# Alternating the two DMA rings between loads and stores, tile by tile, in a split SiLU-multiply kernel

## The chip, the cores and the metric

The kernel runs on one core of one Trainium2 chip. The metric is the device time of one execution in microseconds (us), as the median of several runs; lower is better. Beside the timed runs there is one profiled execution, from which the page of the profile, its views and the record of DMA packets come. Times inside it are counted from the start of its span.

## The reference

The input `x` is a float32 array of 32 x 512 x 2048 (134.22 MB). Each row of 2048 is cut in two halves of 1024; the output is the SiLU of the first half times the second half, in float32, 32 x 512 x 1024 (67.11 MB).

```python
x1, x2 = x[..., :half_dim], x[..., half_dim:]
silu_x1 = x1 * (1 / (1 + np.exp(-x1)))
return (silu_x1 * x2).astype(np.float32)
```

## The kernel before, in words

**Tiling.** The 16384 rows are cut into 16 tiles. A tile has 128 partitions with K = 8 rows each, so a load brings 128 x 16384 floats (8.39 MB) and a whole store takes away 128 x 8192 floats (4.19 MB). A partition's part of a tile is contiguous in the device memory: 64 KB of input and 32 KB of output. In the document `L5` is the load of tile 5 and `S5` its store.

**Buffers.** There are two input buffers, `xt0` and `xt1`, and two output buffers, `ot0` and `ot1`; tile `i` uses number `i % 2` of each. So `L(i+2)` must wait until the multiply of tile `i` has read `xt`, and the multiply of tile `i+2` must wait until `S(i)` has left `ot`.

**Compute.** `compute(i)` issues the SiLU on ScalarE (ACT, L96, in place in the first half of the tile) and then the multiply on VectorE (DVE, L102, into `ot`). Tile 0 is cut into four chunks and tile 15 into three (`LAST`, of 2, 3 and 3 rows); the others are one chunk.

**Transfers.** All of them go through `move` (L77). SyncE (SP) and ScalarE each own a ring on which their DMAs are queued; the page calls the ring of SP q1 and the ring of ACT q10. In the kernel before, every load is issued by SP and every store by ACT. A store on ACT stands in ACT's own instruction stream between the SiLU of its tile and the SiLU of the next tile. `S0` is cut into three pieces by partitions (`OPENING`), and `S15` into three pieces by rows, in step with `LAST`; they are called `S15a`, `S15b` and `S15c` here.

**Order of the work.** The schedule is written out by hand (`manual_schedule`). After `compute(i)` the loop issues `S(i)` and `L(i+2)`, both of which wait for the multiply of tile `i`. Which of the two is written first changes every four tiles (`load_first`); that decides only the order in which the transfers take their eight completion semaphores. At the end `settle_all_but` puts a nop on SP (L67) that waits for the completion of all transfers but the last one, so that what remains after it is the wait for `S15c` and the closing barrier (L160). The calls to `implied` tell the scheduler which dependencies follow from others already waited for.

Of the kernel before, what the change touches and what calls it, by code (L numbers as in the profile page):

```python
# [1 line left out]

# [4 lines left out]


@with_exitstack
def kernel(  # L10
    ctx: ExitStack,
    tc: tile.TileContext,
    x: bass.AP,
    out: bass.AP,
):


    nc = tc.nc
    P = nc.NUM_PARTITIONS

    x_flat = x.flatten_outer_dims()
    out_flat = out.flatten_outer_dims()
    num_rows, in_cols = x_flat.shape
    half = in_cols // 2
    dt = x_flat.dtype

    K = 8
    FIRST = [2] * (K // 2)
    LAST = [2, 3, 3]
    OPENING = [  # L30
        (slice(0, None, 4), slice(None)),
        (slice(2, None, 4), slice(None)),
        (slice(1, None, 2), slice(None)),
    ]
    RUN = 2
    n_tiles = num_rows // (P * K)

    pool = ctx.enter_context(tc.tile_pool(name="pool", bufs=1))
    xts = [pool.tile([P, K, in_cols], dt, name=f"xt{b}") for b in range(2)]
    ots = [pool.tile([P, K, half], dt, name=f"ot{b}") for b in range(2)]  # L40

    def view(flat, i):
        return flat.rearrange("(g p t k) d -> g t p k d", p=P, t=RUN, k=K)[i // RUN, i % RUN]

    ctx.enter_context(tc.manual_schedule(engines={mybir.EngineType.Activation, mybir.EngineType.DVE}))

    sent = []
    loads, stores, silus, muls = {}, {}, {}, {}

    def implied(later, earlier, reason):  # L50
        for x in later:
            for y in earlier:
                tc.declare_no_dep(x, y, reason=reason)

    def earlier(done, i):
        return [ins for j in range(i % 2, i, 2) for ins in done[j]]

    def after(later, first):
        tc.add_manual_dep(
            later,  # L60
            first.name,
            mybir.DependencyInfo(mybir.DependencyClass.NoSync, mybir.DependencyReason.DATA),
            reason="order in which the transfers take their semaphores",
        )

    def settle_all_but(n, others):
        rest = nc.sync.nop(nofuse=True)  # L67
        for ins in sent[:-n] + others:
            tc.add_manual_dep(
                rest.ins,  # L70
                ins.name,
                mybir.DependencyInfo(mybir.DependencyClass.Sync, mybir.DependencyReason.DATA),
                reason="sync sees each earlier transfer land before the last ones",
            )

    def move(queue, out, in_):
        ins = queue.dma_start(out=out, in_=in_).ins  # L77
        sent.append(ins)
        return ins

    def load(i):
        loads[i] = [move(nc.sync, xts[i % 2][:], view(x_flat, i))]
        if i >= 2:
            implied(loads[i], earlier(loads, i), "the multiplies that this load awaits came after those loads")
            implied(loads[i], earlier(silus, i), "the multiplies that this load awaits came after those activations")

    def parts(sizes):
        assert sum(sizes) == K
        return [slice(sum(sizes[:n]), sum(sizes[:n + 1])) for n in range(len(sizes))]

    def compute(i, ot, chunks):
        xt = xts[i % 2]
        silus[i], muls[i] = [], []
        for ks in chunks:
            silus[i].append(
                nc.scalar.activation(  # L96
                    out=xt[:, ks, :half],
                    in_=xt[:, ks, :half],
                    func=mybir.ActivationFunctionType.Silu,
                ).ins  # L100
            )
            muls[i].append(nc.vector.tensor_mul(out=ot[:, ks], in0=xt[:, ks, :half], in1=xt[:, ks, half:]).ins)  # L102
        implied(muls[i], loads[i], "each multiply awaits an activation that came after the load")
        if i >= 2:
            implied(silus[i], earlier(silus, i), "the load that this activation awaits came after those activations")
            implied(silus[i], earlier(muls, i), "the load that this activation awaits came after those multiplies")
            implied(muls[i], earlier(muls, i), "the store that this multiply awaits came after those multiplies")

    def store(i, ot, pieces):
        ov = view(out_flat, i)  # L110
        stores[i] = [move(nc.scalar, ov[ps, ks], ot[ps, ks]) for ps, ks in pieces]

    ALL = slice(None)
    load(0)
    load(1)
    for i in range(n_tiles):
        ot = ots[i % 2]
        last = i == n_tiles - 1
        compute(i, ot, parts(FIRST if i == 0 else LAST if last else [K]))
        pieces = [(ALL, ALL)]  # L120
        if i == 0:
            pieces = OPENING
        elif last:
            pieces = [(ALL, ks) for ks in parts(LAST)]
        load_first = i // 4 % 2
        if load_first and i + 2 < n_tiles:
            load(i + 2)
        store(i, ot, pieces)
        if load_first and i + 2 < n_tiles:
            after(stores[i][0], loads[i + 2][0])  # L130
        if not load_first and i + 2 < n_tiles:
            load(i + 2)
            after(loads[i + 2][0], stores[i][-1])
    settle_all_but(1, muls[n_tiles - 1])


# [1 line left out]
_INS = ['x']  # L138
_OUTS = [((32, 512, 1024), 'float32')]


# [23 lines left out]
```

## Time and profile before

| what | value |
|---|---|
| time, median of 3 runs | 471.06 us (470.71 to 471.17) |
| span of the profiled execution | 469.2 us |
| what lies around the span, as median less span | 1.9 us |
| VectorE busy | 139.5 us (30%) |
| ScalarE busy | 114.2 us (24%) |
| moved by DMA | 201.33 MB, mean 429 GB/s over the span |
| share of 16 DMA engines, ring q1 (loads) and q10 (stores) | 66.4% and 33.2% |
| from issue to landing, whole load and whole store (median) | 42.2 us and 42.0 us |

The profiled execution has no separate time of its own beside the span; the 1.9 us around the span are the difference to the median of the runs. An engine's busy time is a share of the span. A queue's share is the time that its packets took, summed and divided by 16 engines' span, so the two shares together say how full the DMA engines were.

### The profile page before, as it was taken

Reading aid. Unit: us, or ns where it says so; the run is one execution under the profiler, and the core shown is the slowest. Engines: PE = TensorE matmul, PEld = TensorE weight load, DVE = VectorE, ACT = ScalarE, POOL = GpSimd, SP = SyncE. Lnnn points to the kernel's source line nnn. Section 1 sums busy time; section 2 is a strip of 40 time slices with the busy share of each in tenths; the row PEclk is TensorE's granted clock in tenths of the full one; section 3 lists DMA queues with packets and bytes.
Section 4 is the critical chain, followed back from the end, with each engine's and each line's share of the span. In section 5 each row is a group of like instructions: output and inputs, shape, how many; then the busy total and the mean of one; then the engine's idle time right before and its main releaser. Section 6 shows DMA issues by size and latency. Waiting matters only on the chain.

```text
span 469.2 us, 156 instructions
## 1 busy us (share of the span) xinstructions
DVE 139.5 (30%) x21; ACT 114.2 (24%) x22; POOL 0.2 (0%) x4
## 2 busy tenths in 40 slices
DVE  0070522407034070330704307042070520605152
ACT  1051405032050410504105050050501405014060
POOL 0000000000000000000000000000000000000000
DMA  8999999999999999999999999999999999999998
GB/s 358 447 447 374 475 402 433 416 492 402 411 439 486 408 402 447 475 419 402 444 439 458 402 436 413 492 402 416 433 486 408 402 447 475 419 402 444 450 402 358
DMA packets 4928, 201.33 MB, mean 429 GB/s; under 512 B 576, under 2 KB 576, under 8 KB 576
## 3 DMA queue, kind: packets, MB, share of 16 engines
q1 hardware_dynamic: 2304, 134.22, 66.4%
q10 hardware_dynamic: 2624, 67.11, 33.2%
HBM read 134.22 MB, written 67.11 MB: 429 GB/s over the span
## 4 chain that ended last, share of the span: by engine, by line
DMA 72%; DVE 14%; ACT 11%; DVEq 1%; issue 0%; SPq 0%
DMA xt<-in_x_dram 72%; DVE ot L102 14%; ACT xt L96 11%; DVEq L160 1%; SPq L77 0%
## 5 line engine op out<-in xcount | busy, mean ns | idle before, releaser
L102 DVE TENSOR_TENSOR ot<-xt 128x8192 f32<-128x8192 f32 (+2 forms) x21 | 139.5, 6659 | 320.8 <-ACT xt L96 320.8
L96 ACT ACTIVATE xt<-xt 128x8192 f32<-128x8192 f32 (+2 forms) x21 | 112.9, 5400 | 341.4 <-DMA xt<-in_x_dram 341.4
L96 ACT ACT_TABLE_LOAD x1 | 1.3, 1283 | 0.7 <-PEq L149 0.7
L149 POOL MEMSET const-bfloat16-1.0<- 128x1 bf16 x1 | 0.1, 102 | 0.0
L149 POOL MEMSET const-uint8-127<- 128x1 uint8 x1 | 0.1, 102 | 0.0
L149 POOL MEMSET const-float32-0.0<- 128x1 f32 x1 | 0.1, 99 | 0.2 <-issue 0.2
L149 POOL MEMSET const-float32-1.0<- 128x1 f32 x1 | 0.1, 99 | 0.0
## 6 DMA issues: line engine op xcount, KB each, us to landing
out_dram<-ot ACTq DMA_DIRECT2D x14, 4096.0 KB, 42.0
out_dram<-ot ACTq DMA_DIRECT2D x3, 1024.0 KB, 12.0
out_dram<-ot ACTq DMA_DIRECT2D x2, 1536.0 KB, 7.9
out_dram<-ot ACTq DMA_DIRECT2D x1, 2048.0 KB, 37.2
xt<-in_x_dram SPq DMA_DIRECT2D x16, 42.2
```

Source lines behind the costliest of these rows:

```text
L96: nc.scalar.activation(out=xt[:, ks, :half], in_=xt[:, ks, :half], func=mybir.ActivationFunctionType.Silu,).ins
L102: muls[i].append(nc.vector.tensor_mul(out=ot[:, ks], in0=xt[:, ks, :half], in1=xt[:, ks, half:]).ins)
L149: nc = _bacc.Bacc("TRN2", target_bir_lowering=False, num_devices=1)
L160: with _tile.TileContext(nc) as tc:
```

## The change

The helper `load` issues the loads of tiles 3, 5, ..., 15 on ScalarE instead of SyncE, and `store` issues the stores of odd tiles (1, 3, ..., 15, the last in three pieces) on SyncE instead of ScalarE. `L0` and `L1`, the loads of even tiles, and the stores of even tiles stay where they were. For an odd tile's load the declaration about earlier activations falls away, as that load now stands behind those activations on their own engine.

The ring of SP then holds L0, L1, L2, S1, L4, S3, L6, S5, ..., L14, S13, S15a, S15b, S15c, and the ring of ACT holds S0 (three pieces), L3, S2, L5, S4, ..., L15, S14.

```diff
     def load(i):
-        loads[i] = [move(nc.sync, xts[i % 2][:], view(x_flat, i))]
+        loads[i] = [move(nc.scalar if i >= RUN and i % 2 else nc.sync, xts[i % 2][:], view(x_flat, i))]
         if i >= 2:
             implied(loads[i], earlier(loads, i), "the multiplies that this load awaits came after those loads")
-            implied(loads[i], earlier(silus, i), "the multiplies that this load awaits came after those activations")
+            if not i % 2:
+                implied(loads[i], earlier(silus, i), "the multiplies that this load awaits came after those activations")
...
     def store(i, ot, pieces):
         ov = view(out_flat, i)
-        stores[i] = [move(nc.scalar, ov[ps, ks], ot[ps, ks]) for ps, ks in pieces]
+        stores[i] = [move(nc.sync if i % 2 else nc.scalar, ov[ps, ks], ot[ps, ks]) for ps, ks in pieces]
```

## The prediction, made before the changed kernel was run

> **What bounds the kernel now.** I read the page first: the span, the busy shares, and how full the DMA engines are.
>
> ```profile
> span 469.2 us, 156 instructions
> ...
> DVE 139.5 (30%) x21; ACT 114.2 (24%) x22; POOL 0.2 (0%) x4
> ...
> DMA  8999999999999999999999999999999999999998
> ...
> q1 hardware_dynamic: 2304, 134.22, 66.4%
> q10 hardware_dynamic: 2624, 67.11, 33.2%
> ```
>
> No compute engine is busy for a third of the span, while the two rings together fill 66.4 + 33.2 = 99.6% of the 16 DMA engines. The page's chain of waits says "DMA 72%; DVE 14%; ACT 11%", which looks like a latency loop (load, SiLU, multiply, next load). It isn't one that costs anything: the table of windows, over two tiles each, shows full DMA engines at one constant rate while that loop turns.
>
> ```profile
> 116.86:174.86 58.00, 17.38 (x2) 14.06 (x2) 0.00 (x0) 1.00 1.00 434
> 348.86:406.86 58.00, 17.38 (x2) 14.06 (x2) 0.00 (x0) 1.00 1.00 434
> ```
>
> The last columns are the DMA share (1.00) and GB/s (434). Two tiles are 25.17 MB, and 25.17 MB / 58.00 us is 434 GB/s: the period of 29 us a tile is set by bytes. So I looked at single packets. The DMA view of three short windows, each catching one round of 16 packets (one on each engine; the share is summed duration / 16 engines / window, so with a window of 1 us it is the mean duration in units of 0.01 us):
>
> ```profile
> q1 hardware_dynamic: 16, 1.05, 241.8%
> ...
> q10 hardware_dynamic: 16, 0.52, 121.3%
> ...
> q1 hardware_dynamic: 16, 1.05, 328.3%
> ```
>
> The first (48 to 49 us) is a normal load packet: 64 KB in 2.418 us. The second (39.5 to 40.5) is a store packet: 32 KB in 1.213 us. The third (36 to 37) is the round just before the ring of ACT carries its first packet: 3.283 us instead of 2.418, so 0.87 us too long. I come back to it. In the packet record the engines take one load packet and one store packet in turn, 3.62 us a round, from 62 to 448 us without a gap. Packet times add up to 466.6 us an engine, and the DMA engines run from 1.73 to 468.04 us. Nothing is left between packets.
>
> The end, from the timeline:
>
> ```profile
> 435.92 0.34 ACTq L77 DMA_DIRECT2D out_dram<-ot  x1
> 449.08 4.56 ACT L96 ACTIVATE xt<-xt 128x2048 f32<-128x2048 f32 x2 [21.91 <-DMA xt<-in_x_dram]
> ...
> 453.35 0.34 ACTq L77 DMA_DIRECT2D out_dram<-ot  x1
> ...
> 457.07 3.60 ACTq L77 DMA_DIRECT2D out_dram<-ot  x2
> ```
>
> L15 lands at 449.06; S14, S15a, S15b and S15c are issued at 435.92, 453.35, 457.07 and 460.33. In the packet record S14's last packets end at 457.68 to 458.27, S15a's run until about 460.5, S15b's and S15c's until 468.04: each piece is issued 3 us or more before its first packet can go. The end, too, is set by bytes, not by the chain.
>
> **The change, part by part.**
>
> *Issuing instructions.* Seven loads go from SP to ACT, and seven whole stores and three pieces from ACT to SP: SP issues 19 transfers instead of 16, ACT 17 instead of 20. One costs 0.33 us on SP and 0.34 to 0.36 on ACT in the timeline. What hides them is the backlog: L(i+2) and S(i) are issued when L(i+1) and S(i-1) still have 13.1 us to go (L15 lands at 449.06, S14 is issued at 435.92). Without that cover it would be some 0.03 us a tile, 0.5 us in all. I take 0.
>
> *What is queued behind the moved instructions.* On ACT an odd tile's load waits for the multiply (8.69 us) just where the store waited, and behind it stands the next SiLU, whose load lands 13 us later. On SP, S3 waits for the multiply of tile 3, and behind it stands L6, which needs a later multiply anyway. The added waits on older transfers' semaphores (L5 on a piece of S0, for instance) find transfers that landed over 30 us before; an event wait takes 0.02 to 0.03 us in the record. POOL and DVE issue nothing. 0 us.
>
> *The order on the DMA engines.* This is the part that could matter. Each transfer is 8 packets and one semaphore write on each engine, so nine turns, load or store alike. Before, the pairs that share the engines are (L2, S0), (L3, S1), (L4, S2) and so on: L(i+2) and S(i) are issued together, run side by side and land within 0.2 us (L14 at 420.11, S12 at 419.94). After the change L3 stands behind S0 and S1 behind L2; as L2 and S0 end in the same round (72.12 and 71.94), L3 and S1 start together again, and with nine turns on both rings the offset stays the same through the kernel. Every pair is the pair of before, with its rings swapped for odd tiles. Neither ring runs empty before L15 ends. Inside a pair of odd tiles the load's packet now goes ahead of the store's (1.21 us earlier), but its semaphore write takes its turn after the store's last packet, so L15 lands 0.2 us earlier at most, which the backlog swallows. 0 us.
>
> *The end.* S13 ends with L15, near 449 us, and the ring of SP is then empty until S15a is issued at about 453.4, while S14 runs on the ring of ACT with three packets left. From there S14 and S15a take turns, then S15a, S15b and S15c follow. The bytes are the same and both rings hold work, so the last packet again ends near 468.0, unless waking an idle ring costs something: rival 1.
>
> *The nop on SP.* It now stands behind the issue of S15c (460.7) rather than waiting since 409. Its last condition, S15b, lands at 464.74, and S15c at 468.38; its few event waits (0.13 us for the last two) fit in between. Without that cover they would cost about 0.2 us. 0 us.
>
> The sum is 0 for a span of 469.2, and with the 1.9 us around it 471.1 us.
>
> **The rivals.**
>
> *1. Waking an idle ring stalls the engines (slower).* The ring of ACT wakes once in the trace: S0 is issued at 33.5, and the load round before its first packet is stretched by 0.75 to 1.05 us (mean 0.87), though another load packet was queued. The very first packets of the kernel are stretched alike (up to 3.445 us). Before the change there is no other wake. After it, SP's ring is woken by S15a in a stretch where the engines have no slack, so the whole stall goes into the end: 471.06 + 0.87 = 471.9, at most 472.1. For it: the only wake in the trace shows it. Against it: the stall may belong to the first use of a ring or to the first write in the kernel, and both happen alike in both kernels. [...]
>
> *2. Mixing directions on one ring costs something at each change (slower).* Before, each ring carries one direction only, so the trace can't show a load behind a store on the same ring. What it shows is that engines change direction at every packet for nothing (2.418 and 1.213 us throughout), and that the turn from one pair to the next costs 0.01 to 0.02 us (rounds of 3.63 and 3.64 against 3.62). After the change, 14 such turns change direction on a ring. It decides from 0.94 / 14 = 0.07 us a turn on. At the stall of rival 1 each time it would be 14 x 0.87 = 12 us, 483 us; at a tenth of that 1.2 us, 472.3. The bound below is 0: a turn can't get cheaper than the 0.02 us that it costs.
>
> *3. Faster.* That would need shorter packets, since start (1.73 us), end (1.15 us) and the two stretched rounds lie outside what is changed. Taking 0.2% off means 5 ns of each 2418 ns packet, perhaps because on a ring that alternates the read of the next packet meets the write of the one ahead less often; 470.1. Nothing in the trace varies by that much: 1926 of 2048 load packets took 2.418 us to the nanosecond. [...]
>
> That the change doesn't do what it says can be put aside: the instruction streams built from it hold the rings as listed above.
>
> **How the numbers follow.** No change, 471.1 us (470.5 to 471.7): 0.54. Rival 1, 471.9 to 472.1: 0.26. Rival 2, from 472.0 up: 0.14. Rival 3: 0.06. A difference of 0.2%, 0.94 us, is about the least that a measurement of this kernel can tell from none. Rival 1 at 0.75 to 1.05 us lies across that bound, so I split it in halves: within 0.2% is 0.54 + 0.13 = 0.67, slower is 0.13 + 0.14 = 0.27, faster 0.06. The range takes the forecast with its spread (the runs spread by 0.46 us), rival 1, and rival 2 up to a tenth of its price with the same spread: 470.4 to 472.6.
>
> **What would show it.** If right: packets of 2.418 and 1.213 us throughout, L15 landing near 449, the last packet ending near 468.0. Rival 1 would show as one stretched round near 454 us and an end near 469. Rival 2 would show as stretched packets every 29 us, at the turn between pairs, and periods above 58.0 us in the windows of two tiles. A DMA share below 1.00 in those windows would mean that a ring ran empty, and the whole argument on pairs would be wrong.

## The result, and the profile after

The changed kernel takes 486.53 us (median of 4 runs, 485.46 to 488.05) against 471.12 us before: 3.3% slower, ratio 1.0333, 95% interval 1.0321 to 1.0345. The forecast was 471.1 us with a range up to 472.6.

The page of the changed kernel; the columns are those of the page before.

```profile
span 483.7 us, 163 instructions
...
DVE 139.5 (29%) x21; ACT 114.2 (24%) x22; POOL 0.2 (0%) x4
...
DMA  9999999999999999999999999999999999999997
...
q1 hardware_dynamic: 2736, 109.05, 53.9%
q10 hardware_dynamic: 2192, 92.28, 44.9%
```

Compute is what it was, to a tenth of a microsecond. The DMA engines are nearly as full as before, 53.9 + 44.9 = 98.8% of a span that is 14.5 us longer, with the same bytes. So they hardly stood idle for want of work: packets took longer, 477.7 us an engine in all against 466.6. The table of windows shows two stretches of time that the prediction shows too (start and end, length, busy time of DVE, ACT and POOL, clock, DMA share, GB/s):

```profile
116.86:174.86 58.00, 15.56 (x3) 14.06 (x2) 0.00 (x0) 1.00 1.00 424
348.86:406.86 58.00, 17.39 (x2) 11.41 (x3) 0.00 (x0) 1.00 0.99 415
```

Busy 1.00 and 0.99, but 424 and then 415 GB/s instead of 434. So the DMA share of 1.00 was here no proof that bytes moved at the rate of before; the last column showed that they did not.

Where the time goes is seen in the DMA view of one window of 2.9 us, from 99.9 us on, in which each engine takes one load packet (64 KB) and one store packet (32 KB). First the kernel before, then the changed one:

```profile
q1 hardware_dynamic: 32, 1.05, 83.7%
q10 hardware_dynamic: 32, 0.52, 42.1%
```

```profile
q1 hardware_dynamic: 32, 1.05, 113.1%
q10 hardware_dynamic: 32, 0.52, 51.3%
```

The share times the window is the mean duration: 0.837 x 2.9 = 2.43 us for the load packet before (with its 4-byte semaphore write, 9 ns in the packet record), 1.131 x 2.9 = 3.28 us after; the store packet goes from 1.22 to 1.49 us. That is 1.1 us an engine, at the moment when the pair (L3, S1) gives way to (L4, S2). At the turn before it, near 71 us, where L2 and S0 give way to L3 and S1, nothing is stretched in the packet record. From then on it happens at every second turn, as the SiLUs of ScalarE show (start and duration first; those of tiles 3, 4, 5, 6, 14 and 15):

```profile
101.37 7.03 ACT L97 ACTIVATE xt<-xt 128x8192 f32<-128x8192 f32 x1 [22.18 <-DMA xt<-in_x_dram]
131.97 7.03 ACT L97 ACTIVATE xt<-xt 128x8192 f32<-128x8192 f32 x1 [23.57 <-DMA xt<-in_x_dram]
161.19 7.03 ACT L97 ACTIVATE xt<-xt 128x8192 f32<-128x8192 f32 x1 [22.19 <-DMA xt<-in_x_dram]
193.11 7.03 ACT L97 ACTIVATE xt<-xt 128x8192 f32<-128x8192 f32 x1 [24.88 <-DMA xt<-in_x_dram]
...
434.30 7.03 ACT L97 ACTIVATE xt<-xt 128x8192 f32<-128x8192 f32 x1 [23.23 <-DMA xt<-in_x_dram]
463.45 7.22 ACT L97 ACTIVATE xt<-xt 128x2048 f32<-128x2048 f32 x3 [22.12 <-DMA xt<-in_x_dram]
```

Before the change they start at 101.08, 130.14, 159.08, 188.13, 420.14 and 449.08. The delay is 0.29 us at tile 3, 1.83 at tile 4, 2.11 at tile 5, 4.98 at tile 6, and 14.37 at tile 15. Over the whole list, the six even tiles 4 to 14 add 11.73 us between them (1.2 to 2.9 each) and the odd tiles 5 to 15 only 2.35. The rest of the span, from tile 15's SiLU on, is 20.2 us against 20.1.

I call the two kinds of turn by what meets at them. At the turn to an odd tile the packets on an engine go `S0 L2 | L3 S1`: load packets meet. At the turn to an even tile they go `L3 S1 | S2 L4`: store packets meet, and there the first load packet is late.

### The profile page after: what moved, and what is told of

It is laid out like the page before. It is cut to its first block, busy times and chain, and to the rows that moved or that the text cites. A ratio compares the mean times of both kernels' runs of the same rounds, so it can differ in the third digit from the quotient of the medians.

```text
span 483.7 us, 163 instructions
## 1 busy us (share of the span) xinstructions
DVE 139.5 (29%) x21; ACT 114.2 (24%) x22; POOL 0.2 (0%) x4
## 3 DMA queue, kind: packets, MB, share of 16 engines
q1 hardware_dynamic: 2736, 109.05, 53.9%
q10 hardware_dynamic: 2192, 92.28, 44.9%
## 4 chain that ended last, share of the span: by engine, by line
DMA 73%; DVE 13%; ACT 11%; DVEq 1%; ACTq 1%; issue 0%; SPq 0%
DMA xt<-in_x_dram 73%; DVE ot L103 13%; ACT xt L97 11%; DVEq L161 1%; ACTq L161 1%; SPq L77 0%
```

## The experiments

I had four guesses for a stall of some 1.2 us: two store packets in a row, the semaphore writes between them, a ring that changes direction, or something that needs both rings. The first three kernels separate these.

**One piece of S0.** The kernel before with the first store in one transfer.

```diff
-    OPENING = [
-        (slice(0, None, 4), slice(None)),
-        (slice(2, None, 4), slice(None)),
-        (slice(1, None, 2), slice(None)),
-    ]
+    OPENING = [(slice(None), slice(None))]
```

> The kernel before with S0 as one transfer instead of three pieces. The rings stay pure (loads on SP, stores on ACT), but S0 then has 9 turns on the engines instead of 11, so that the stores run two turns ahead of the loads, and at the end of every load its semaphore write falls between two store packets: store, semaphore, store, load, 14 times. Theory A (two store packets in a row leave an engine without a load read under way, and the next load packet pays for it): 14 stalls of about 1.1 us, some 486 us. Theory B (a semaphore write straight after a store packet waits for that packet's write): the same, about 486 us. Theory C (a ring that changes between load and store pays at the change): no ring changes, so 471 us, up to 1.4 us more for the later start of the stores.

Measured 470.83 us, ratio 1.0000 (0.9991 to 1.0009). The DMA view of the window 100.9 to 104.3 us, with one load packet and two store packets of each engine in it:

```profile
q1 hardware_dynamic: 32, 1.05, 71.4%
q10 hardware_dynamic: 32, 1.05, 71.4%
```

0.714 x 3.4 = 2.43 us is one load packet on q1 and exactly two unstretched store packets on q10, which are neighbours in the packet record, with a semaphore write between. Theories A and B fall: neither neighbouring store packets nor a semaphore write behind one cost anything on these pure rings.

**Rings exchanged once.** From tile 3's load and tile 1's store on, loads go on ACT and stores on SP.

```diff
-        loads[i] = [move(nc.sync, xts[i % 2][:], view(x_flat, i))]
+        loads[i] = [move(nc.scalar if i >= 3 else nc.sync, xts[i % 2][:], view(x_flat, i))]
...
-        stores[i] = [move(nc.scalar, ov[ps, ks], ot[ps, ks]) for ps, ks in pieces]
+        stores[i] = [move(nc.sync if i >= 1 else nc.scalar, ov[ps, ks], ot[ps, ks]) for ps, ks in pieces]
```

> The rings are exchanged once and then stay pure: loads from tile 3 on go on ACT, stores from tile 1 on go on SP. In each pair the load's packet then goes ahead of the store's, so a pair ends with load, store, semaphore, semaphore, load, store: the semaphore writes come straight after a store packet at 13 boundaries, but no two store packets are neighbours. Theory A: no stall, 471 us. Theory B: 13 stalls of about 1.1 us, some 485 us. Theory C: one change of each ring, 471 to 472.3 us.

Measured 471.35 us, ratio 1.0010 (1.0001 to 1.0019). No stall, so B falls a second time. Which ring carries the loads made about 0.1% of difference, 0.5 us. In the window 99.9 to 102.8 us the load packet, now on q10, takes 0.837 x 2.9 = 2.43 us:

```profile
q10 hardware_dynamic: 32, 1.05, 83.7%
```

**One pair.** As above, with `i == 3` and `i == 1` as the conditions, so that only L3 and S1 change their rings.

> The kernel before with only L3 on ACT and S1 on SP; everything else as before. One even-odd boundary (load, semaphores, load) near 71 us and one odd-even boundary (store, semaphores, store) near 100 us. All of theories A, B and C: one stall of about 1.1 us at 100 us, 472.2 us. If seven such boundaries cost 15 us only because the engines drift apart and each later stall grows, a single one must cost no more than 1.2 us and leave no stretched packet behind it; if the cost comes from the rings having been mixed at all, stretched packets go on after 130 us and the time is well above 473 us.

Measured 472.52 us, ratio 1.0033 (1.0021 to 1.0045): 1.64 us for one load and one store that change rings for one tile. The window 99.9 to 102.8 us:

```profile
q1 hardware_dynamic: 32, 1.05, 115.7%
q10 hardware_dynamic: 32, 0.52, 53.2%
```

The load packet takes 3.36 us, the store packet 1.54: 1.25 us an engine. After that no packet is stretched. So the cost of the exchanged pair was in this one turn, and the stall didn't go on by itself. Theories A, B and C all foresaw it, so this run alone doesn't choose between them.

The next three ask what the turn needs.

**The changed kernel with S0 in two pieces.**

```diff
-    OPENING = [
...
-    ]
+    OPENING = [(slice(n, None, 2), slice(None)) for n in range(2)]
```

> The changed kernel with S0 in two pieces instead of three: 10 turns instead of 11, so one ring runs a turn ahead of the other for the rest of the kernel. Counted in turns, a ring that changes direction (load to store, or store to load) then always has at least 2.43 us of the other ring's packets between its last packet of the one kind and its first of the other; with three pieces that cover is 2.43 us at the even-odd turn and 1.22 us at the odd-even one, where the stalls are. Theory D (a ring needs some 2.4 us from its last packet in one direction to its first in the other, and the engine stands still for what the other ring doesn't cover): the stalls go, 471 to 473 us, though all 27 changes of direction and 20 neighbouring pairs of store packets are there. Theory E (a change of ring together with two neighbouring store packets costs): still 14 us or more slower, 485 us or above. Theory F (only the change from store to load on SP's ring, or load to store on ACT's, costs, whatever lies between): 485 us.

Measured 481.41 us, ratio 1.022 (1.017 to 1.027). It lies between the theories: theory D's 471 to 473 us is missed by 8 us, and E and F by 4. Two store packets of the other ring now lie between a ring's last store packet and its first load packet. The window 101.2 to 104.5 us holds the first such turn:

```profile
q1 hardware_dynamic: 32, 1.05, 89.6%
q10 hardware_dynamic: 16, 0.52, 37.0%
```

The load packet takes 0.896 x 3.3 = 2.96 us, stretched by 0.53 us instead of 0.85, and the store packet 1.22, not stretched. Later turns stretch packets on some engines by up to 1.8 us, and the next SiLU waits for the engine that is last. The trace holds sixteen completion marks (semaphore updates) for each transfer, one for each engine; in the changed kernel those of L3 lie between 100.36 and 101.35 us, and tile 3's SiLU starts at 101.37. In this run the middle one of L15, their median, comes 2.6 us later than before the change, but the last four come 4 to 6.5 us behind the middle one. So two store packets between bring twelve of the engines near to what theory D said, and the time still goes by the four that lose most.

**The changed kernel with S0 in four pieces.** As above, with step 4 and `range(4)`.

> The changed kernel with S0 in four pieces: 12 turns, so the order in a round is reversed, and the cover is 1.22 us at the even-odd turn (SP from load to store, ACT from store to load, the first time near 72 us) and 2.43 us at the odd-even turn. Theory D: the stalls move to the even-odd turn; seven of them at about 1.2 us and some drift, 480 to 487 us, with stretched packets near 72 and 130 us and none at 100 and 159 us. Theory E: stalls where store packets are neighbours across a change. Theory F: stalls stay at 100 and 159 us.

Measured 488.2 us, ratio 1.0361 (1.0339 to 1.0383). The stalls did move. The window 71.0 to 73.9 us, at the turn to tile 3, where nothing was stretched in the changed kernel:

```profile
q10 hardware_dynamic: 31, 1.05, 116.0%
q1 hardware_dynamic: 30, 0.52, 54.9%
```

The load packets are those of L3 on ACT's ring now, 3.36 us on average. In the packet record turns near 130 and 190 us follow, and those at 100 and 159 us are free. So the stall isn't tied to SP's ring, nor to the tile: it follows the order of the packets. Theory F falls.

**Everything on one ring.**

```diff
-        stores[i] = [move(nc.scalar, ov[ps, ks], ot[ps, ks]) for ps, ks in pieces]
+        stores[i] = [move(nc.sync, ov[ps, ks], ot[ps, ks]) for ps, ks in pieces]
...
-        load_first = i // 4 % 2
+        load_first = False
```

> The kernel before with every transfer on SP's ring, the store always issued before the load (load_first always false): one ring changes direction 28 times with nothing on the other ring to cover it. The engines have 13 us of backlog at each issue, so that without a price of changing the time stays 471 us. Theory D: each change exposes its full turnaround. If only store to load costs 2.4 us: 14 x 2.4 = 34 us more, 505 us; if both directions do: 538 us; the stretched packets show which. Theory E (needs both rings): 471 us. Theory F: 14 changes from store to load at about 1.2 us, 488 us.

Measured 476.21 us, ratio 1.0112 (1.0097 to 1.0127). Theory D wanted 505 or 538 us, theory F 488, and theory E's 471 is missed by 5. One turn from stores to loads, in the window 80.9 to 82.0 us:

```profile
q1 hardware_dynamic: 32, 1.05, 222.4%
```

That is 2.224 x 1.1 = 2.45 us for the load packet and a semaphore write. Over the run there are 224 such turns on single engines (14 turns on 16 engines), and at 222 of them the first load packet took its 2.418 us; at the other two it took 0.1 and 0.2 us more. On one ring, going from stores to loads cost nothing at those 222 turns, and theory C falls. The 5 us come elsewhere: the last load packet before a turn to stores is stretched on a few engines, by up to 1.1 us. All the stretching after the first turn adds up to 1.2 us an engine, but it falls on few of them: the middle completion mark of L15 comes 0.6 us later than before, only four of the sixteen are more than 1 us behind that, and the last one comes 4.8 us later than before.

So the stall of 1.25 us was seen only with the other ring at work. The next kernels look for how it takes part.

**Halves on both rings.** Every transfer is cut in two by partitions, one half on each ring; the store is always issued first, and S0 is in one piece.

```diff
+    HALVES = [(nc.sync, slice(0, 64)), (nc.scalar, slice(64, 128))]
...
-        loads[i] = [move(nc.sync, xts[i % 2][:], view(x_flat, i))]
+        loads[i] = [move(q, xts[i % 2][ps], view(x_flat, i)[ps]) for q, ps in HALVES]
...
-        stores[i] = [move(nc.scalar, ov[ps, ks], ot[ps, ks]) for ps, ks in pieces]
+        stores[i] = [move(q, ov[ps, ks], ot[ps, ks]) for _, ks in pieces for q, ps in HALVES]
```

> Each load and each store is cut in two halves of 64 partitions, one half on SP's ring and one on ACT's, with the store always issued before the load. Both rings are active and both mix directions, 28 times each, but they turn together: both go from store to load at the same time and from load to store at the same time, with nothing of the other kind between. Theory D (a ring that turns needs some 2.4 us, and the engine waits for what the other ring doesn't cover): no cover at all, 14 to 28 stalls of about 2.4 us, 505 us or above. Theory G (the stall needs opposed turns: one ring going to loads as the other goes to stores; rings that turn together, or a single ring, read ahead across the turn): like the single ring, 471 to 477 us.

Measured 705.43 us (693.45 to 718.96). Neither theory foresaw that, and it has nothing to do with turning: load packets are slow from the first load on. In a window of 1.2 us, 60.8 to 62.0, with one load packet on each engine, a packet takes 4.110 x 1.2 = 4.93 us (the median of the whole run is 4.32):

```profile
q1 hardware_dynamic: 16, 1.05, 411.0%
```

Only loads are slow: 4.93 us a packet against 2.418 in the kernel before, while store packets stayed at 1.21 us in the median. Why, this run does not show. This kernel says nothing on turns, so the next one cuts the halves differently.

**Halves by even and odd partitions.** The rest is as in the kernel with halves.

```diff
-    HALVES = [(nc.sync, slice(0, 64)), (nc.scalar, slice(64, 128))]
+    HALVES = [(nc.sync, slice(0, None, 2)), (nc.scalar, slice(1, None, 2))]
```

> The halves again, cut by even and odd partitions instead of lower and upper 64. In the first version load packets took about 4.9 us instead of 2.418 from the first load on, long before any ring turned, while store packets took 1.21 us: that slowness belongs to the way the loads were cut and not to turning. If it came from all engines writing into one half of the partitions at a time, the even-odd cut removes it, load packets take 2.418 us, and the time shows what turning together costs: theory G (opposed turns are needed) 471 to 477 us, theory D (any ring that turns) 500 us or above. If it comes from two rings carrying loads side by side on one engine, load packets stay at 4 to 5 us and the time near 700 us.

Measured 476.4 us, ratio 1.0114 (1.0097 to 1.0131), the single ring's time. The window 61.7 to 62.7 us: load packets are back at 2.418 us.

```profile
q1 hardware_dynamic: 16, 1.05, 241.8%
```

The rings turn together here, and the median first load packet of either ring is late by 0.00 us (some 200 of 224 turns could be followed on each). Rings that turned together didn't stall at the turn. The 5.5 us are again mostly with a few engines: the middle completion mark of L15 comes 1.6 us later than before, the last one 5.2.

**The changed kernel with S0 in eight pieces.** As with two pieces, with step 8 and `range(8)`.

> The changed kernel with S0 in eight pieces: 16 turns instead of 11, so that the rings turn at different times. Counted in turns, at the odd-even turn SP goes from store to load and ACT from load to store with about 4.8 us of the other ring's packets in between, and at the even-odd turn from the second one on with 2.4 us (ACT, store to load) and 4.85 us (SP, load to store). With two pieces the cover at the odd-even turn was 2.43 us, and the first stall there 0.54 us instead of 1.16. Theory D: no stretched packets at 100 us or 159 us, small ones (0.5 us) at 130 and 188 us, 475 to 479 us. Theory G with any opposed turn costing whatever lies between: seven to fourteen stalls of 0.5 to 1.2 us, 480 to 488 us. If nothing but neighbouring turns in one round costs: 471 to 473 us.

Measured 486.84 us, ratio 1.0332 (1.0273 to 1.0391), outside theory D's 475 to 479 and inside theory G's 480 to 488. Part of it is the cut itself: between 44 and 57 us the packets of S0 and of the load beside it are stretched by 4.5 us an engine in all, two thirds of it on stores. There are no stalls near 100 and 130 us (theory D wanted none at 100 and a small one at 130), but from 190 us on there are stalls on most engines. The engines had lost step in the opening: by 111 us the completion marks of one transfer lie 5 us apart. So the agreement with G's number says little, and as an experiment this run decides little.

**One ring turns, the other doesn't.** The output of tile 1 is stored by SP and once more by ACT (to the place of tile 15's output, which S15 overwrites).

```diff
-        stores[i] = [move(nc.scalar, ov[ps, ks], ot[ps, ks]) for ps, ks in pieces]
+        stores[i] = [move(nc.sync if i == 1 else nc.scalar, ov[ps, ks], ot[ps, ks]) for ps, ks in pieces]
+        if i == 1:
+            stores[i].append(move(nc.scalar, view(out_flat, n_tiles - 1), ot[:]))
```

> The kernel before with S1 on SP's ring, and the output of tile 1 stored a second time by ACT at the same moment, to the place of tile 15's output, which S15 overwrites at the end. So between about 71 and 90 us both rings carry stores; then SP's ring turns from S1 to L3 while ACT's ring goes on from store to store (S2). The only direct turn from store to load has one store packet of the other ring between, as at the odd-even turn of the changed kernel, but the other ring doesn't turn. The extra store is 4.19 MB, 9.65 us at 434 GB/s: 480.8 us without a stall. If the turning ring alone pays (theory D): the first load packet after it, near 92 us, is stretched together with the store packet before it by about 1.3 us, 482 us. If both rings must turn against each other (theory G): no stretched packet there, 480.8 us.

Measured 482.84 us, ratio 1.0253 (1.0232 to 1.0273). S2's first packet came too late: the first load packet of L3 followed S1's last store packet directly, and it wasn't stretched. In the window 90.3 to 93.2 us it takes 0.837 x 2.9 = 2.43 us with a semaphore write:

```profile
q1 hardware_dynamic: 32, 1.05, 83.7%
```

The number is theory D's 482 all the same, but the 2 us above 480.8 lie later. ACT's ring has run empty, and when it is woken by S3 (issued at 136.09) load packets are stretched on a few engines near 138 and 148 us; one engine loses 2.7 us over three of them, and its completion marks come some 2.6 us behind the middle one from then to the end. The condition I wanted wasn't met, so I filled ACT's ring for longer:

```diff
-            stores[i].append(move(nc.scalar, view(out_flat, n_tiles - 1), ot[:]))
+            stores[i] += [move(nc.scalar, view(out_flat, n_tiles - n), ot[:]) for n in (1, 3)]
```

> In e10 ACT's ring was empty at the turn (S2 came 1 us too late), so SP's ring turned from S1 to L3 with nothing of the other ring between. Here the output of tile 1 is stored twice more by ACT, to the places of tiles 15 and 13, which their own stores overwrite later, so that ACT's ring still carries stores when SP's ring turns, near 90 us: store on SP, semaphore writes, store on ACT, first load on SP, as at the odd-even turn of the changed kernel, but ACT's ring comes from a store and not from a load. The extra stores are 8.39 MB, 19.3 us at 434 GB/s: 490.4 us without a stall. Theory G (rings must turn against each other): no stretched packet near 92 us. Theory D' (one store packet of the other ring between a ring's last store and its first load is enough): the first load packet there stretched by about 1.2 us.

Measured 490.85 us, ratio 1.0421 (1.039 to 1.0451), against 490.4 us without a stall. The window 90.4 to 93.0 us holds the turn:

```profile
q1 hardware_dynamic: 32, 1.05, 94.9%
q10 hardware_dynamic: 32, 0.52, 48.2%
```

0.949 x 2.6 = 2.47 us for the load packet and 1.25 for the store packet: 0.07 us in place of 1.2. The packets are store, store, load, on the same rings as at the bad turn; only ACT's ring comes from a store and not from a load. This is the pair of runs on which the verdict rests: with the kernel of one pair, a ring that went from stores to loads stalled where the other went from loads to stores (1.25 us), and didn't where the other kept to stores (0.07 us). Both figures come from one profiled execution each, on all 16 engines. No run has the other ring keep to loads at such a turn, so it is not shown whether it must itself turn, or whether a load packet of it just ahead is enough.

**Blocks of four tiles.** Last, a count that the theory gives beforehand.

```diff
+    def swapped(i):
+        return i in (3, 4, 5, 6, 11, 12, 13, 14)
...
-        loads[i] = [move(nc.sync, xts[i % 2][:], view(x_flat, i))]
+        loads[i] = [move(nc.scalar if swapped(i) else nc.sync, xts[i % 2][:], view(x_flat, i))]
...
-        stores[i] = [move(nc.scalar, ov[ps, ks], ot[ps, ks]) for ps, ks in pieces]
+        stores[i] = [move(nc.sync if swapped(i + 2) else nc.scalar, ov[ps, ks], ot[ps, ks]) for ps, ks in pieces]
```

> The kernel before with the rings exchanged in blocks of four tiles: L3 to L6 and L11 to L14 on ACT, with S1 to S4 and S9 to S12 on SP; all else as before. 28 of the 54 transfers change their ring, as many as in the changed kernel, but the rings turn against each other only four times: twice with load packets meeting (at L3 and L11) and twice with store packets meeting (at L7 with S5, and at L15 with S13). If only a turn at which store packets meet costs (theory G), two stalls as in the run with one pair (472.5 against 470.9, so 1.6 us each): 474.2 us, stretched packets near 217 and 450 us only. If every turn costs alike, four of them: 477 us. If it is the number of transfers on the other ring that costs: 480 us or above.

Measured 474.26 us, ratio 1.0072 (1.0058 to 1.0086), against a forecast of 474.2. (The count in the expectation is wrong: 16 of 36 transfers change their ring, against 17 in the changed kernel. And the two stalls stand at 188 and 421 us, where L7 and L15 start; the times named there are about where these land.) The windows 187.1 to 190.0 and 420.2 to 423.3 us:

```profile
q1 hardware_dynamic: 32, 1.05, 116.2%
q10 hardware_dynamic: 32, 0.52, 51.9%
```

```profile
q1 hardware_dynamic: 32, 1.05, 108.4%
q10 hardware_dynamic: 32, 0.52, 51.2%
```

The load packets take 3.37 and 3.36 us, and nothing is stretched at the two turns where load packets meet. Nearly as many transfers change their ring as in the changed kernel, at a fifth of its price: what counts is how often the rings turn against each other with store packets meeting, 2 times here and 6 there.

The packet record doesn't name the engines, but on an engine a packet starts 3 to 4 ns before the one ahead of it ends (4873 of 4912 times in the kernel before), so packets can be followed from one to the next, until the engines are too far out of step. In the changed kernel, its variants with two and four pieces, and the kernels with rings exchanged once, for one pair and in blocks, I looked at the first load packet of a ring that had carried a store. With one store packet of the other ring between, it ends late by 1.23 us (median of 169); with two, by 0.34 (68, nearly all in the kernel with two pieces); with load packets between, by 0.00 (186).

## Why the prediction was wrong

**What held.** The bound was read rightly: bytes on the DMA engines, and the loss there went into the end whole: L15 lands 14.4 us later, and the span is 14.5 us longer. Issue, waits and the nop cost nothing that shows: from S15c's landing to the end of the span it is 0.8 us in both kernels. The pairs stay together as worked out: L3 and S1 land at 101.35 and 101.53. No ring ran empty before L15 ended.

**The step that failed** is "the order on the DMA engines", with its sum of 0. It treated pairs as equal when the same packets go in the same turns, whichever ring they come from. They are not: at the opposed turn at 100 us the first load packet took 2.8 to 3.8 us in place of 2.418. The term that I put at 0 measures 14.4 us up to tile 15's SiLU: 0.3 at tile 3, 11.7 at the six turns where store packets meet, 2.4 at the others.

**Rival 2** had the right place and the wrong mechanism. It charged every change of direction on a ring, 14 turns; in the single ring (222 of 224 turns) and the even-odd halves (0.00 us in the median) a ring's own change from stores to loads brought no stall, and the full price fell at 6 turns out of 14. Its 12 us (14 x 0.87) is near the measured 14.4 by chance: 6 x 1.96 = 11.7, and the rest from elsewhere. What should have been kept was its far end. The text said that the trace could not show a load behind a store on a ring, and then cut the range at a tenth of the price, with no row that gave the tenth. "Engines change direction at every packet for nothing" was a row about something else: there each ring kept to its own direction.

**Rival 1** is not what slowed this kernel. Four of 16 engines show a packet stretched by 0.8 to 1.0 us when S15a wakes SP's ring near 469 us, 0.23 us an engine, and from tile 15's SiLU to the end the span is 0.1 us longer. So this wake didn't bring the stall of all 16 engines that the kernel before shows at 36 us (0.87 us). But another wasn't free: in the kernel with one ring turning, the wake at 138 us stretched packets on a few engines, and that run lost 2 us; the slowest engine's completion marks came some 2.6 us behind the middle one to the end.

**Rival 3**: no load packet took less than 2.415 us, and the time went up instead: which ring carries a transfer made 15 us of difference here.

**What stays open.** Why the load packet comes late at such a turn is not shown: these runs can't see into an engine. A first turn cost 1.1 us an engine in the changed kernel, 1.25 with one pair, and 1.5 to 1.8 us of landing, later ones up to 2.9; in the later half some load packets on ACT's ring in the middle of a pair are stretched too (0.3 to 0.7 us an engine, near 260, 273, 328, 383 and 445 us). The engines did fall out of step: the sixteen completion marks of a load lie within 0.5 to 0.7 us throughout the kernel before, and in the changed kernel within 1.0 us at L3, 3.4 at L7 and 5.4 at L13. But that is not most of the loss: the middle mark of L15 comes 12.5 us later than before, the last one 14.4. That the lost step is why later turns cost more is likely, but only argued.

## What to carry to other kernels

When the DMA engines are full, as here, keep each ring to one direction; exchanging the rings once cost about 0.5 us, and alternating them tile by tile 15. A price that the trace can't show keeps its full end in the range, whatever the argument for zero. And a DMA share of 1.00 stood here beside 434 GB/s and beside 424: compare GB/s and the duration of one packet. The transfers here are spread over all engines and the slowest ones set the time (with S0 in two pieces the middle completion mark of L15 came 2.6 us late, the last four 4 to 6.5 us behind it), so look at their packets and not at the mean alone.

## What the runs showed that I had not expected

- Two rings that turned against each other cost 1.2 to 2.9 us a turn where store packets met, 1.64 us in the run with a single one. Rings that turned together, or a single ring with all transfers, cost 5 us over 28 changes of direction, most of it on a few slow engines.
- Loads in two halves of 64 neighbouring partitions, one on each ring, took 4.93 us a 64 KB packet in one window (4.32 in the median of the run) and the kernel 705 us; even and odd partitions took 2.418 us and 476 us.
- Each semaphore write (4 bytes, 9 ns in the packet record) took a turn of its own between the rings, so the number of pieces of the first store (9, 10, 11 or 12 turns) set the order of the packets for the rest of the kernel: with the changed rings 481 us with two pieces and 488 us with four, with pure rings no difference between one and three.
